# A two-layer hybrid trunk step: x laid out turned and loaded by token groups, squares summed by products with ones, first projections by groups, other ranks of the woven jobs

## The chip, the cores and the metric

The kernel runs on one core of one Trainium2 chip. The metric is device time in microseconds (us) of that core, for one execution of the whole program. Times of a kernel are given as the median of several runs, with the lowest and highest. Traces come from one profiled execution.

## The reference, cut to what matters

One inference step of a trunk of two layers, for a prompt of 1024 tokens and 8 samples of 4 tokens each, so T = 1056 tokens of width D = 1024.

```python
for layer in range(2):
    shift, scale, gate = split(silu(c) @ w_mod[layer] + b_mod[layer])       # c: prompt row, 8 sample rows
    h = rms_norm(x, norm_g[layer]) * (1 + scale) + shift
    if layer == 0:   # sliding-window attention: 16 heads, 4 KV heads of 64, window 128, sinks
        q, k, v, z = split(h @ swa_w_in)
        branch = (attend(q, k, v) * silu(z)) @ swa_w_out
    else:            # gated DeltaNet: 8 q/k heads, 16 v heads of 128, conv of 4 taps, chunks of 64
        xqkv, z, a, b = split(h @ gdn_w_in)
        q, k, v = silu(causal_conv(xqkv))                                    # q, k then l2-normalised
        o = gated_delta(q, k, v, beta(b), decay(a), S0)                      # a state S per head and sample
        branch = (rms_norm(o) * silu(z)) @ gdn_w_out
    x = x + gate * branch
y = rms_norm(x, final_norm_g)
```

Outputs are y, the last keys and values, and the new conv and DeltaNet states.

## The kernel before, in words

**Layout.** Activations lie turned: the width stands on the 128 partitions, in 8 slices (KD = 8, numbered k or e), and the tokens on the columns, in three token groups (`GRP`, L24): columns 0 to 384, 384 to 768, and 768 to 1056, the last 32 of these being the sample tokens. An fp32 product of full precision is made of three products in the faster type fp32r, since each factor is split into a high and a low part: hi·hi, hi·lo and lo·hi (`hhi`, `hlo` of the activations; `wh`, `wl` of the weights).

**Who sets the order.** All instructions go through one helper (`call`, L83), so the profile shows L84 for nearly all of them. The program order on each engine is the order in which the Python code issues them; a planner keeps a model of when each engine comes free (`nc.free`). Loads that must keep an order among themselves go through `queued` (L276) on SyncE's queue (SP). Work that is not on the main line (attention, the chunks of DeltaNet, the splitting of weights, the sample tokens) is written as generators, "jobs". `weave` (L456) puts a job into a list by its rank from the tables `K` and `KR` (lower rank first), and `stages` (L467) tries the list from the front between two matrix products of the main line; a job goes on until its next condition does not hold. So a changed rank changes what stands between which products, not what is computed. `MM` (used at L1243) spaces the steps of the second layer's modulation, `SW` (used at L2378) the products with the sample states S.

**The front** (L282 to L735). `xload` brings x, as it is stored, in nine blocks of up to 128 tokens (512 KB each) into `xt`. `turn_x` (L605) turns a block by eight 128x128 transposes on TensorE, copies the result into `zo` (the turned x) on VectorE and has ScalarE square the block and add up each token's squares (`xss`). The pool of `xt` has `XB` = 14 places, shared with the modulation weights `wm` (eight slices, two loads of 512 KB each, `wmod_load`). `modulation_rows` shapes the conditioning vector `cT`; `modulate(e)` (L638) makes slice e of shift and scale by eight 32-row products with `wm`; `fold(e)` (L649) turns the result to columns, `Sc` and `Sh`. `scale_x` (L618) makes the reciprocal root of all nine blocks at once in small VectorE steps (`sv` to `rsx`); `spread_x(gi)` (L624) spreads it over the partitions by products with the identity and has ScalarE copy it to `rsb`. `hold(n)` (L673) issues n filler products whose result is not used. `shape_h(k)` (L657) makes slice k of the layer's input: `fu` = x · Sc · rsb on VectorE, `hhi` = fu + Sh on ScalarE, `hlo` = the remainder on VectorE, in two spans of prompt columns, and four small steps for the 32 sample columns. `split_w` (L420) makes `wh` on ScalarE, then `wl` on GpSimd. `first_part(k, p_)` (L685) makes slice k's nine products for one of two column blocks, 3 groups by 3 products; 8 slices, 2 column blocks and 9 products are the 144 first projections. The loop over k that issues them computes slice k+1's `shape_h` beside slice k's products and loads weights ahead.

**The middle.** Layer 0's other projections (`project`, L519) with attention woven in; its output product; layer 1's projections with the chunked DeltaNet woven in.

**The last stage** is layer 1's output product, in blocks (`out_block`, L2259) of 48 products of 512 columns, 768 in all, on `h2hi`, `h2lo` (activations) and `ohi`, `olo` (weights). Woven between them is the samples' DeltaNet, a chain: 16 steps with S (`states_times`, L2349: four 32x256 products `S,zq` each, two loads of 512 KB for each step ahead through five places), then `core` (L2403: KQT, U, oH), then `second_half` and `new_states` (L2586, L2601: `U,kb`). The sample rows' own block comes behind the 384th output product.

Of the kernel before, what the change touches and what calls it, by code (L numbers as in the profile page):

```python
# [14 lines left out]
P = 128  # L15
D = 1024
# [198 lines left out]
def body(tc, I, O, cst_ap, dbg=None):  # L215
# [21 lines left out]
    K = {'split': 4, 'add': 3, 'attend': 12, 'turning': 14, 'modulate': 31, 'cached': 9, 'wo': 39, 'turn': 0, 'ahead': 2, 'taps': 2, 'gating': 5, 'decay': 27, 'samples': 9, 'load': 4, 'mod': 9, 'shape': 9, 'decays': 8, 'prepare': 0, 'gather': 30, 'finish': 55, 'states': 21, 'core': 4, 'new': 9}  # L237
    KR = [{'chain': 8, 'output': 3, 'solve': 5, 'invert': 21, 'blocks': 10, 'decayed': 0}, {'chain': 10, 'output': 3, 'solve': 12, 'invert': 10, 'blocks': 35, 'decayed': 40}, {'chain': 33, 'output': 2, 'solve': 22, 'invert': 19, 'blocks': 33, 'decayed': 9}, {'chain': 20, 'output': 21, 'solve': 3, 'invert': 4, 'blocks': 30, 'decayed': 17}, {'chain': 14, 'output': 0, 'solve': 1, 'invert': 17, 'blocks': 31, 'decayed': 11}, {'chain': 3, 'output': 13, 'solve': 6, 'invert': 20, 'blocks': 55, 'decayed': 29}, {'chain': 6, 'output': 1, 'solve': 11, 'invert': 20, 'blocks': 45, 'decayed': 11}, {'chain': 10, 'output': 8, 'solve': 4, 'invert': 28, 'blocks': 40, 'decayed': 44}]
    TB = (3, 6)
    SW = (1, 16)  # L240
# [3 lines left out]
    MM = (0, 20)  # L244
# [4 lines left out]
    XB, FB = 14, 3  # L249
    FH, LATEP = (1, 3), False  # L250
# [11 lines left out]
    gb = cp.tile([P, 64], F32, name="gb")  # L262
# [22 lines left out]
    xts, wms = {}, {}  # L285
# [11 lines left out]
    early = COFF["fold32"][0] + COFF["fold32"][1]  # L297
    cst = cp.tile([P, nkeep], F32, name="cst")
    C = {k: cst[:, o:o + w] for k, (o, w) in COFF.items() if o < nkeep}
    ident = C["ident"]  # L300
    craw = xp.tile([P, KD, 9], F32, name="craw")
    xload(0)
    queued(cst[:, 0:early], cst_ap[:, 0:early])
    xload(1)
    queued(craw.rearrange("p k c -> p (k c)"), I["cgb"][:, 64:136])
    queued(gb, I["cgb"][:, 0:64])
    turns_x = [0, 1, NB, 2, 3, 4, 5, 6, 7]
    for t in turns_x[2:]:
        xload(t)
# [2418 lines left out]
```

## Time and profile before

| | before |
| --- | --- |
| runs, us | 1671.0, 1672.88, 1670.3 (median 1671.0) |
| the profiled execution's own time, us | 1669.87 |
| its span in the trace, us | 1668.1 |
| mean granted TensorE clock | 0.988 |
| instructions in the trace | 30471 |
| HBM read, written | 147.54 MB, 49.84 MB: 118 GB/s over the span |

How to read the lines that follow. In the page, an engine's row gives busy us, the share of the span, and the number of instructions; PEld is the weight load of TensorE, which overlaps its products. In the busy times by stretches, a row has the stretch, its length, then the busy us (and the instructions) of PE, PEld, DVE, ACT and POOL, the granted TensorE clock, the mean busy share of the 16 DMA engines, and the GB/s that they moved. In the rows in order of time stand the start, the duration in us, the engine, the line, the operation with what it writes and reads, the shape, the number of trace records, and in square brackets the idle time of the engine just ahead of the row and what ended it. Where one row stands for several products, its start is that of the first, and a fp32 product that isn't split counts two records.

### The profile page before, as it was taken

The page shows a single profiled execution, that of the slowest core. Times are in us where ns is not written, and L with a number is a line of the kernel's source. Part 1 is how long each engine was busy: PE and PEld are TensorE (multiplying, and loading weights), DVE is VectorE, ACT ScalarE, POOL GpSimd, SP SyncE. Part 2 cuts the span into 40 slices and gives each one's busy share as a digit, 9 for nine tenths or more (in the row PEclk, how much of TensorE's full clock was granted, in tenths as well). Part 3 has the DMA queues.
Part 4 walks back from the last instruction along what each step waited for, and adds up shares of the span by engine and source line. Part 5 has one row for each costly group of instructions (what it writes and reads, how often), then busy time and mean ns, then how long its engine had stood idle before and what let it go on. Part 6 is the DMA issues. An engine that isn't in the chain of part 4 may idle for free.

```text
span 1668.1 us, 30471 instructions
## 1 busy us (share of the span) xinstructions
PE 1594.5 (96%) x10552; PEld 1411.4 (85%) x10552; DVE 1224.1 (73%) x3809; ACT 844.8 (51%) x2422; POOL 221.8 (13%) x289
## 2 busy tenths in 40 slices
PE   8999999999999999989999999999999999888896
PEld 6888888978678999979999889999999987466775
DVE  6726776665666687887988878787898967277777
ACT  4635565444344664546653754656655745133332
POOL 1300000003222001020010102001010033132231
PEclk9999999999999999999999999999999999998998
DMA  9442111124332423133313224232242157853784
GB/s 353 142 142 77 56 49 51 64 72 141 108 128 96 125 61 97 48 104 93 110 51 101 82 74 118 65 113 71 68 132 55 62 167 200 262 192 121 243 271 154
DMA packets 190891, 196.80 MB, mean 118 GB/s; under 512 B 86432, under 2 KB 137472, under 8 KB 190688
## 3 DMA queue, kind: packets, MB, share of 16 engines
q1 hardware_dynamic: 190736, 194.84, 38.0%
q8 instruction: 84, 1.38, 0.3%
q14 instruction: 71, 0.58, 0.1%
HBM read 147.54 MB, written 49.84 MB: 118 GB/s over the span
## 4 chain that ended last, share of the span: by engine, by line
PE 49%; DVE 8%; DMA 4%; ACT 3%; issue 1%; POOL 0%; SPq 0%; POOLq 0%; ACTq 0%; DVEq 0%
PE ps_pj L84 31%; PE ps_lg L84 7%; PE ps_mi L84 6%; PE ps_ob L84 3%; PE ps_tr L84 3%; DMA S<-in_states 1%; DMA of<-gTd 1%; DVE rst L84 1%; DVE y L84 1%; DVE S L84 1%; DVE rsw L84 0%; ACT L84 0%; DVE oH L84 0%; ACT jc L84 0%; DMA xt<-x2d 0%
## 5 line engine op out<-in xcount | busy, mean ns | idle before, releaser
L84 PE MATMUL ps_pj<-h2lo,wh 128*128 128x384 f32 (+1 forms) x1128 | 379.8, 337 | 0.0
L84 PE MATMUL ps_pj<-h2hi,wl 128*128 128x384 f32 (+1 forms) x1128 | 378.4, 335 | 0.9 <-DVE wl L84 0.9
L84 PE MATMUL ps_pj<-h2hi,wh 128*128 128x384 f32 (+1 forms) x1128 | 378.4, 335 | 0.0
L84 PEld LDWEIGHTS ps_pj<-h2hi,wl 128*128 128x128 f32 x1128 | 212.5, 188 | 4.1 <-DVE wl L84 1.2
L84 PEld LDWEIGHTS ps_pj<-h2hi,wh 128*128 128x128 f32 x1128 | 212.5, 188 | 2.9
L84 PEld LDWEIGHTS ps_pj<-h2lo,wh 128*128 128x128 f32 x1128 | 212.4, 188 | 2.8
L84 POOL TENSOR_TENSOR Xd<-Xc,cst 32x128 f32<-32x128 f32 x128 | 68.0, 531 | 425.3 <-DMA Xc<-Xdd 195.7
L84 PE MATMUL ps_pj<-hlo,wh 128*128 128x384 f32 (+1 forms) x376 | 124.3, 331 | 0.1
L84 PE MATMUL ps_pj<-hhi,wh 128*128 128x384 f32 (+1 forms) x376 | 124.4, 331 | 0.0
L84 PE MATMUL ps_pj<-hhi,wl 128*128 128x384 f32 (+1 forms) x376 | 123.4, 328 | 0.0
L84 DVE TENSOR_TENSOR wl<-wr,wh 128x512 fp32r<-128x512 f32 x120 | 83.2, 693 | 16.1 <-ACT wh L84 15.5
L84 POOL TENSOR_TENSOR xt<-xt,y 128x512 f32<-128x512 f32 (+1 forms) x48 | 65.4, 1364 | 219.6 <-DVE y L84 199.5
L84 DVE SCALAR_TENSOR_TENSOR vT<-XR,cT,vT 128x384 f32<-128x384 f32 (+1 forms) x144 | 80.8, 572 | 10.4 <-ACT vT L84 9.6
L84 ACT CAST wh<-wr 128x512 fp32r<-128x512 f32 x128 | 78.6, 616 | 16.4 <-PE ps_pj L84 14.8
L84 PEld LDWEIGHTS ps_pj<-hlo,wh 128*128 128x128 f32 x376 | 70.7, 188 | 11.2 <-issue 10.2
L84 PEld LDWEIGHTS ps_pj<-hhi,wh 128*128 128x128 f32 x376 | 70.7, 188 | 4.1 <-issue 3.8
L84 PEld LDWEIGHTS ps_pj<-hhi,wl 128*128 128x128 f32 x376 | 70.7, 188 | 2.8 <-issue 2.7
L84 DVE TENSOR_TENSOR X<-X,tmp 128x126 f32<-128x126 f32 (+22 forms) x248 | 63.8, 257 | 8.5
L84 ACT ACTIVATE qe<-ps_mi,Eg 128x128 f32<-128x128 f32 x112 | 35.0, 363 | 68.8 <-PE ps_mi L84 68.8
L84 ACT COPY XR<-ps_pj 128x384 f32<-128x384 f32 (+1 forms) x96 | 43.3, 451 | 52.1 <-PE ps_pj L84 51.8
L84 DVE TENSOR_TENSOR tmp<-X 128x126 f32<-128x126 f32 (+22 forms) x248 | 62.3, 251 | 7.7 <-POOL X L84 3.9
L84 ACT ACTIVATE prob<-prob,nm 128x256 f32<-128x256 f32 (+1 forms) x128 | 62.2, 488 | 9.6 <-DVE nm L84 9.4
(542 smaller groups left out, 3910.9 us busy)
## 6 DMA issues: line engine op xcount, KB each, us to landing
wr<-in_gwb SPq DMA_DIRECT2D x96, 256.0 KB
S<-in_states SPq DMA_DIRECT2D x40, 256.0 KB
xt<-in_x_prompt SPq DMA_DIRECT2D x16, 512.0 KB
wm<-in_wm SPq DMA_DIRECT2D x16, 512.0 KB
wr<-in_winb SPq DMA_DIRECT2D x32, 256.0 KB
wmod<-in_w_mod SPq DMA_DIRECT2D x32, 256.0 KB
wm<-in_w_mod SPq DMA_DIRECT2D x32, 256.0 KB
DP<-gcr SPq DMA_DIRECT2D x64, 128.0 KB
```

The lines of the kernel that those rows point to most:

```text
L84: inst = fn(*args, **kwargs)
```

## The change

It has three parts, and nothing else differs.

**The front's data.** The host lays x out turned, in two arrays: `xT0` (the first two token groups, four loads of two slices each, 786 KB) and `xT1` (the third group, two loads of four slices). They are loaded straight into `zo`; the transposes, their copies and `xt` as a place of x are gone. The early constants, the norm and bias rows and the conditioning vector come as one load, `erl`. The pool that is now of `wm` alone has 12 places.

**The front's work.** `square_x` squares slices of the turned x, odd ones on VectorE and even ones on ScalarE; `total` sums them over the partitions by products with a column block of ones (`w32`), each into one of four 32-row strips; `scale_tot` copies the sums, and `scale_x` makes 1/32 of the strips' sum by products of one column, six blocks of tokens at first and three later, and then the reciprocal root as before. `shape_h` takes a range of columns, and its `hlo` half is issued separately (`rest`); the sample columns have `shape_s`. `first_part` takes the groups it is to do, and its order is hi·hi, lo·hi, hi·lo. The loop over k gives way to a list written out by hand: groups 0 and 1 of the first slices ahead of group 2. Of the two calls of `hold`, with one and three products, the first stays.

**The ranks.** Six entries of `K`, six of `KR`, `SW` and `MM` have other values.

```diff
-    K = {'split': 4, ... 'cached': 9, ... 'load': 4, ... 'shape': 9, ... 'states': 21, ... 'new': 9}
+    K = {'split': 25, ... 'cached': 29, ... 'load': 6, ... 'shape': 5, ... 'states': 14, ... 'new': 4}
...
-    SW = (1, 16)
+    SW = (4, 19)
-    MM = (0, 20)
+    MM = (1, 17)
-    XB, FB = 14, 3
-    FH, LATEP = (1, 3), False
+    XB, FB = 12, 4
...
-    def xload(t):
-        xts[t] = xp.tile([P, D], F32, tag="xt", name="xt", bufs=XB)[0:P if t < NB else TS]
-        queued(xts[t], xp_rows[t * P:(t + 1) * P] if t < NB else xs_rows)
+    def xload(gi, i):
+        w = zo[0].shape[1] // (2 - gi)
+        queued(zo[i * w // 4][:, i * w % 4:i * w % 4 + w, (0, 2 * GW)[gi]:(2 * GW, T)[gi]], I[f"xT{gi}"][i])
...
-    def turn_x(n, t):
...
-                nc.tensor.transpose(pt[:, j * parts:(j + 1) * parts], xts[t][:, k * P:(k + 1) * P],
-                                    ident[0:parts, 0:parts])
-            nc.vector.tensor_copy(zo[kk][:, :, t * P:t * P + parts],
-                                  pt[:, 0:4 * parts].rearrange("p (q t) -> p q t", q=4))
-        nc.scalar.activation(sq[0:parts], xts[t], AF.Square, accum_out=xss[0:parts, n:n + 1])
+    def square_x(q, gis):
+        a, b = GRP[gis[0]][0], GRP[gis[-1]][1]
+        sqs = {}
+        for e in (2 * q, 2 * q + 1):
+            x = zo[e // 4][:, e % 4, a:b]
+            sqs[e] = xp.tile([P, 2 * GW], F32, tag="sq", name="sq", bufs=4)[:, 0:b - a]
+            if e % 2:
+                nc.vector.tensor_tensor(sqs[e], x, x, ALU.mult)
+            else:
+                nc.scalar.activation(sqs[e], x, AF.Square)
+        def total():
+            for gi in gis:
...
+                for e, sq in sqs.items():
+                    j = (e + 2 * gi) % 4
+                    nc.tensor.matmul(sums[gi][32 * j:32 * j + 32, 0:b1 - a1], w32[:, 0:32], sq[:, a1 - a:b1 - a],
+                                     start=(e < 4), stop=(e >= 4), skip_group_check=True)
...
+    def scale_x(gis):
...
+            nc.tensor.matmul(pss[0:n, j:j + 1], tot[:, t * P:t * P + n], w32[:, 32:33], start=True, stop=True)
...
-            for n, (x, y) in enumerate(((hi, hhi), (hi, hlo), (lo, hhi))):
+        for n, (x, y) in enumerate(((hi, hhi), (lo, hhi), (hi, hlo))):
+            for gi in gis:
...
+    scale_tot((0, 1))
+    scale_x((0, 1))
+    hold(1)
+    modulate(0)
+    fws[0] = split_w(fraws.pop(0))
+    fold(0)
+    spread_x(0)
+    spread_x(1)
+    shape_h(0, 0, 768)
+    us.pop((0, 0))()
+    modulate(1)
+    wmod_load(6)
+    square_x(0, (2,))
+    first_part(0, 0, (0, 1))
+    square_x(1, (2,))
+    fold(1)
+    shape_h(1, 0, 768)
+    fws[1] = split_w(fraws.pop(1))
+    totals[0, 2]()
+    modulate(2)
...
```

What stands on the engines now. First TensorE at its start. In before, this is what follows sixteen groups of transposes of x like the first two rows (`cst` holds the identity):

```order
L84 MATMUL ps_tr<-cst,xt 128x128 x4
L84 MATMUL ps_ob<-cst,xt 128x128 x4
L84 MATMUL ps_mi<-wm_122,cT 32x256 x4
L84 MATMUL ps_mi<-wm_124,cT 32x256 x4
L84 MATMUL ps_mi<-wm_128,cT 32x256 x4
L84 MATMUL ps_mi<-wm_130,cT 32x256 x4
L84 MATMUL ps_mi<-cst,ma 128x32 x2
L84 MATMUL ps_mi<-zo,cst 128x384
L84 MATMUL ps_lg<-cst,rsx 128x128 x3
L84 MATMUL ps_ob<-cst,rsx 128x128 x3
L84 MATMUL ps_lg<-cst,rsx 128x128 x2
L84 MATMUL ps_lg<-cst,rsx 128x32
```

In after, the same engine's first instructions are these (`sq` are the squares, `w_98` the ones, `erl` holds the identity):

```order
L84 MATMUL ps_lg<-sq,w_98 32x384 x16
L84 MATMUL ps_tr<-w_98,tot 128x1 x6
L84 MATMUL ps_mi<-zo,erl 128x384
L84 MATMUL ps_mi<-wm_107,cT 32x256 x4
L84 MATMUL ps_mi<-wm_109,cT 32x256 x4
L84 MATMUL ps_mi<-erl,ma 128x32 x2
L84 MATMUL ps_ob<-erl,rsx 128x128 x3
L84 MATMUL ps_tr<-erl,rsx 128x128 x3
L84 MATMUL ps_mi<-wm_113,cT 32x256 x4
L84 MATMUL ps_mi<-wm_115,cT 32x256 x4
L84 MATMUL ps_pj<-hhi,wh 128x384 x2
L84 MATMUL ps_pj<-hhi,wl 128x384 x2
```

The 72 transposes are replaced by sixteen sums and six one-column products; only one modulation stands ahead of the spread, which covers two token groups, and a projection of two groups follows the second modulation.

Second, SyncE's queue at the start, in before (`craw` and `gb` are the conditioning vector and the norm and bias rows):

```order
L84 DMA xt<-in_x_prompt 128x1024
L84 DMA cst<-in_cst 128x160
L84 DMA xt<-in_x_prompt 128x1024
L84 DMA craw<-in_cgb 128x72
L84 DMA gb<-in_cgb 128x64
L84 DMA xt<-in_x_sample 32x1024
L84 DMA xt<-in_x_prompt 128x1024 x6
L84 DMA wm_122<-in_wm 128x1024
L84 DMA wm_124<-in_wm 128x1024
L84 DMA wr<-in_win 128x512
L84 DMA wm_128<-in_wm 128x1024
L84 DMA wm_130<-in_wm 128x1024
```

And the same queue in after:

```order
L84 DMA zo<-in_xT 128x2x768
L84 DMA erl<-in_erl 128x296
L84 DMA zo<-in_xT 128x2x768 x3
L84 DMA wm_107<-in_wm 128x1024
L84 DMA wm_109<-in_wm 128x1024
L84 DMA wr<-in_win 128x512
L84 DMA wm_113<-in_wm 128x1024
L84 DMA wm_115<-in_wm 128x1024
L84 DMA wm_117<-in_wm 128x1024
L84 DMA wm_119<-in_wm 128x1024
L84 DMA zo<-in_xT 128x4x288 x2
L84 DMA cst<-in_cst 128x488
```

The weights of the first two modulations now stand behind two token groups of x instead of three, and the third group behind the weights of slice 2.

Third, TensorE in the last stage, where the products with S begin. In before (`h2hi`, `h2lo`, `ohi`, `olo`: output products; a row of `S,zq` is half a step):

```order
L84 MATMUL ps_pj<-h2hi,ohi 128x512
L84 MATMUL ps_lg<-S_17060,zq 32x256 x2
L84 MATMUL ps_lg<-S_17062,zq 32x256 x2
L84 MATMUL ps_pj<-h2hi,olo 128x512
L84 MATMUL ps_lg<-S_17064,zq 32x256 x2
L84 MATMUL ps_lg<-S_17066,zq 32x256 x2
L84 MATMUL ps_pj<-h2lo,ohi 128x512
L84 MATMUL ps_pj<-h2hi,ohi 128x512
L84 MATMUL ps_pj<-h2hi,olo 128x512
L84 MATMUL ps_pj<-h2lo,ohi 128x512
```

In after:

```order
L84 MATMUL ps_pj<-h2hi,olo 128x512
L84 MATMUL ps_lg<-S_17051,zq 32x256 x2
L84 MATMUL ps_lg<-S_17053,zq 32x256 x2
L84 MATMUL ps_lg<-S_17055,zq 32x256 x2
L84 MATMUL ps_lg<-S_17057,zq 32x256 x2
L84 MATMUL ps_pj<-h2lo,ohi 128x512
L84 MATMUL ps_tr<-erl,vo 128x128 x4
L84 MATMUL ps_pj<-h2hi,ohi 128x512
L84 MATMUL ps_pj<-h2hi,olo 128x512
L84 MATMUL ps_pj<-h2lo,ohi 128x512
```

Two steps with S stand back to back in after. Counted in output products ahead of each of the 16 steps, before has 97, 98, 106, 107, 116, 121, 125, 160, 163, 167, 172, 176, 181, 185, 190, 194, and after 98, 98, 104, 105, 116, 116, 149, 149, 157, 158, 166, 167, 175, 176, 184, 190. The transposes of KQT stand behind 283 output products in before and 277 in after, the first product of U with `kb` behind 358 and 352, the product of `oH` behind 384 in both; from the 482nd on the rows are the same.

On GpSimd two memsets of the attention's cached values stand behind the front in after and not at the start, since the memory that they write is the front's until then. From about 600 to 1350 us TensorE's rows are nearly the same in both kernels, and the number of instructions is close everywhere: TensorE's queue has 8977 in before and 8935 in after, VectorE's 3811 and 3822, ScalarE's 1991 and 1997, GpSimd's 294 and 297, SyncE's 973 and 968.

More of the change, by code (lines that the diff above doesn't have):

```diff
@@ L695, in body @@
     wmod_load(1)
-    for n, t in enumerate(turns_x):
-        turn_x(n, t)
-        if n == 1:
-            modulation_rows()
-    queued(cst[:, early:], cst_ap[:, early:nkeep])
     wmod_load(2)
+    xload(1, 0)
+    xload(1, 1)
+    queued(cst, cst_ap[:, early:nkeep])
     first_load(1)
-    ma = modulate(0)
-    scale_x(0, 9)
-    ma1 = modulate(1)
-    fold(0, ma)
-    fws[0] = split_w(fraws.pop(0))
-    hold(FH[0])
-    for gi in range(3):
-        spread_x(gi)
-    shape_h(0)
-    fold(1, ma1)
```

255 lines of the change are left out of this document (182 added, 73 removed).

## The prediction

> **What bounds the kernel now.** I read the share of busy time first, then the busy time by stretches, then TensorE's rows in order of time, and last the rows of the engines it waits for.
>
> ```profile
> PE 1594.5 (96%) x10552; PEld 1411.4 (85%) x10552; DVE 1224.1 (73%) x3809; ACT 844.8 (51%) x2422; POOL 221.8 (13%) x289
> ...
> 0.00:10.00 10.00, 4.21 (x20) 3.51 (x20) 2.33 (x4) 4.66 (x8) 2.44 (x11) 1.00 0.84 273
> 10.00:20.00 10.00, 9.77 (x71) 8.88 (x70) 8.34 (x15) 7.19 (x15) 0.04 (x1) 1.00 1.03 407
> 20.00:30.00 10.00, 8.79 (x51) 6.37 (x51) 5.17 (x20) 3.62 (x8) 2.72 (x3) 0.83 1.03 406
> 30.00:40.00 10.00, 9.92 (x78) 7.62 (x77) 9.35 (x21) 4.44 (x11) 1.38 (x1) 1.00 0.98 383
> 40.00:50.00 10.00, 10.00 (x83) 8.51 (x83) 9.07 (x22) 4.27 (x9) 1.38 (x1) 1.00 0.14 44
> ...
> 100.00:150.00 50.00, 50.00 (x359) 44.12 (x358) 30.55 (x120) 24.14 (x80) 0.00 (x0) 1.00 0.31 108
> ```
>
> TensorE (PE) is busy for 1594.5 of 1668.1 us, and from 100 us on a stretch is 50.00 of 50.00: whatever the front saves is kept behind it, since the work there is limited by TensorE and merely starts earlier. In the front the last two columns matter: for 40 us the DMA engines are full at about 0.407 MB/us (2.73 MB in the first 10 us), and TensorE's busy time there is partly filler and transposes. So the price of the change is read from one question: when do the real projections start, and how long do they then take?
>
> ```profile
> 20.57 0.64 PE L84 MATMUL ps_mi<-wm,cT 128*32 128x256 f32 x8 [0.80 <-DMA wm<-in_wm]
> 21.85 0.64 PE L84 MATMUL ps_mi<-wm,cT 128*32 128x256 f32 x8 [0.64 <-DMA wm<-in_wm]
> ...
> 22.98 1.65 PE L84 MATMUL ps_mi<-zo,cst 128*128 128x384 f32 x2
> 24.42 1.49 PE L84 MATMUL ps_lg<-cst,rsx 128*128 128x128 f32 x6
> 26.71 0.94 PE L84 MATMUL ps_lg<-cst,rsx 128*128 128x128 f32 x6
> 28.05 2.18 PE L84 MATMUL ps_mi<-zo,cst 128*128 128x384 f32 x6
> 29.78 0.63 PE L84 MATMUL ps_pj<-hhi,wh 128*128 128x384 f32 x1
> 30.48 0.44 PE L84 MATMUL ps_pj<-hlo,wh 128*128 128x384 f32 x1
> ...
> 45.94 1.07 PE L84 MATMUL ps_mi<-wm,cT 128*32 128x256 f32 x16
> 50.47 1.07 PE L84 MATMUL ps_mi<-wm,cT 128*32 128x256 f32 x16
> ...
> 62.91 0.40 PE L84 MATMUL ps_tr<-hlo,wh 128*128 128x288 f32 x1 [0.45 <-DVE hlo L84]
> 64.61 0.30 PE L84 MATMUL ps_ob<-hhi,wl 128*128 128x288 f32 x1
> ```
>
> The first projection stands at 29.78 and the last of the sixteen (eight slices of the model width, two column blocks) ends at 64.91, so 35.1 us. Inside, one slice takes 4.53 us (45.94 to 50.47) with almost no wait named. Two of the rows ahead of it, 22.98 and 28.05 (the products of zo with the identity), are filler from `hold`.
>
> **The change part by part: when the first projection starts.** The loads first. In before, the second half of the modulation weights of slice 1 stands behind 6.83 MB in the queue; at 0.407 MB/us these have moved by 10 + (6.83 - 2.73) / 0.407 = 20.1 us, and the row at 21.85 starts when it lands: 1.8 us behind the count. In after, the first two token groups of x (four loads of 128x2x768) and the early constants are 3.30 MB, so they land at 11.4 + 1.8 = **13.2 us**; the weights of slice 1 (5.66 MB) at 19.0, the third group (7.89 MB) at 24.5, the last modulation weights (14.15 MB) at 39.9. All but the first lie ahead of their use below, so the DMA sets only the start.
>
> From 13.2 us a chain follows, priced by the nearest rows:
>
> ```profile
> 4.73 1.09 PE L84 MATMUL ps_pj<-cst,xt 128*128 128x128 f32 x4 [4.73 <-DMA cst<-in_cst]
> 17.73 0.60 PE L84 MATMUL ps_tr<-cst,xt 128*128 128x128 f32 x4
> ...
> L84 DVE TENSOR_TENSOR wl<-wr,wh 128x512 fp32r<-128x512 f32 x120 | 83.2, 693 | 16.1 <-ACT wh L84 15.5
> ...
> 20.24 0.16 DVE L84 TENSOR_SCALAR sv<-xss 128x9 f32<-128x9 f32 x1
> 22.49 0.17 DVE L84 SCALAR_TENSOR_TENSOR rsx<-rst,rsw 128x9 f32<-128x9 f32 x1
> 26.46 0.62 DVE L84 SCALAR_TENSOR_TENSOR fu<-zo,Sc,rsb 128x384 f32<-128x384 f32 x1 [2.89 <-ACT rsb L84]
> ...
> 22.55 0.37 ACT L84 COPY ma<-ps_mi 128x256 f32<-128x256 f32 x1 [2.35 <-PE ps_mi L84]
> 25.95 0.48 ACT L84 COPY rsb<-ps_lg 128x384 f32<-128x384 f32 x1 [2.50 <-PE ps_lg L84]
> ```
>
> The last square on 768 columns of VectorE (DVE) is 1.5 times the 693 ns row, 1.0 us. The products with ones were not in before. Four of them work on separate 32-row strips, as the modulation's do (the 20.57 row: 0.64 us for four of 256 columns), so 0.96 us for 384 columns, 1.9 at the half clock. Copy of the sums 0.48. Six products with one column are bounded by the transposes, which load the same 128x128 operand: 0.9 (17.73 row) to 1.6 (4.73 row). Then the branches: on VectorE the reciprocal root, 20.24 to 22.66, 2.4 us; on TensorE one filler product (0.7 to 1.65), modulation 0 (1.07 to 2.1), ScalarE's copy 0.37, the fold (0.6 to 1.0). TensorE's branch is the longer one. After it the spread (0.94 to 1.49), its copy 0.48, the scaling 0.62 and the bias on ScalarE, about 0.62 more. At the full clock the sum is 13.2 + 1.0 + 0.96 + 0.48 + 0.9 + (0.73 + 1.07 + 0.37 + 0.63) + 0.94 + 0.48 + 0.62 + 0.62 = **22.0**; at half the clock **26.6**. The 72 transposes, which cost TensorE from 4.73 to 18.8 us, are gone, but they lay beside the loads, so they count only through this chain. I take 24.0: cold for the sums, warm for about half of the rest. That is 5.8 us ahead of 29.78.
>
> **How long the projections then take.** The same 144 projection products, six modulations and the folds take 35.1 us in before. Added between them: one fold (0.4), eight sums over 288 columns, two side by side (four times 0.72, of which two pairs stand together: 2.2), three one-column products (0.4) and the spread of the third group (0.5), 3.5 us. Lost are the two stalls seen above, 30.48 - 29.78 instead of 0.18 and 0.45: 1.0 us. Sum 37.6 us, so the front ends at 24.0 + 37.6 = **61.6**.
>
> VectorE is the second bound, and here it is as near:
>
> ```profile
> 31.24 0.28 DVE L84 TENSOR_SCALAR Sc<-ps_mi,bS,gb 128x9 f32<-128x9 f32 x1
> 34.68 1.29 DVE L84 TENSOR_TENSOR hlo<-fs,hhi 128x32 fp32r<-128x32 f32 x1
> 35.89 0.28 DVE L84 TENSOR_SCALAR Sc<-ps_mi,bS,gb 128x9 f32<-128x9 f32 x1
> 39.33 0.18 DVE L84 TENSOR_TENSOR hlo<-fs,hhi 128x32 fp32r<-128x32 f32 x1
> 40.00 0.28 DVE L84 TENSOR_SCALAR Sc<-ps_mi,bS,gb 128x9 f32<-128x9 f32 x1 [0.49 <-PE ps_mi L84]
> ...
> 34.54 1.38 POOL L84 TENSOR_TENSOR wl<-wr,wh 128x512 fp32r<-128x512 f32 x1 [4.92 <-ACT wh L84]
> ```
>
> A slice is 4.65 us (31.24 to 35.89) where GpSimd (POOL) splits a weight meanwhile, and 4.11 - 0.49 = 3.62 where it doesn't: four of each, 33.1 us. Added are four squares of 288 columns (0.39 each, 1.6), a second reciprocal root (2.4) and 16 more instructions, since the columns come in three pieces and not in two (an estimate of 1.0); taken away are three of the four small sample steps of slices 0 to 3 (1.4). From the first scaling at about 22.8 that is 36.7 us, so 59.5, and 2.1 us of projections follow the last slice: 61.6 again. Two engines with the same sum mean that a stall on either is no longer covered, so no more than this is taken: **-3.3 us** against 64.91, with ends at -5.3 (first product at 22.0, end 59.6) and -0.5 (every GpSimd product blocks VectorE, below).
>
> The rows at 34.54 and 34.68 show VectorE's small difference (0.18 us at 39.33) held up until GpSimd's product ends. The Trainium skill's page "SBUF — State Buffer" says of the shared port pair that a VectorE operation with two SBUF inputs and a GpSimd operation that reads SBUF exclude each other, and the second fully blocks; this row agrees. By that rule the squares and the root's steps, which have two such inputs, would be held up as well. With it the sum is the first rival's, 1669.1; without it, 1666.3.
>
> **The rest.** The multiset of the other instructions is unchanged; from about 600 to 1350 us TensorE's order is nearly word for word the same, so nothing is booked there. The ranks move work in the attention part (both signs open, booked at 0 with 2 either way) and in the last stage:
>
> ```profile
> 1414.83 0.39 PE L84 MATMUL ps_pj<-h2hi,olo 128*128 128x512 f32 x1
> 1415.06 0.39 PE L84 MATMUL ps_pj<-h2lo,ohi 128*128 128x512 f32 x1
> ...
> 1424.47 1.30 PE L84 MATMUL ps_lg<-S,zq 128*32 128x256 f32 x8 [2.48 <-DMA S<-in_states]
> 1435.43 0.63 PE L84 MATMUL ps_lg<-S,zq 128*32 128x256 f32 x4 [1.16 <-DMA S<-in_states]
> 1527.75 0.63 PE L84 MATMUL ps_lg<-cst,oH 128*128 128x128 f32 x4 [2.60 <-DVE oH L84]
> ...
> 1420.00:1440.00 20.00, 16.31 (x85) 9.19 (x86) 4.68 (x14) 3.06 (x9) 1.48 (x2) 0.91 0.90 281
> ```
>
> Of the 768 output products, 384 stand ahead of the product of oH in both kernels, and TensorE waits there 2.60 us for the sample chain. In after the chain's earlier members stand six output products sooner (the KQT transposes behind 277 of them, not 283; the first product of U behind 352, not 358). One is 0.23 us (1414.83 to 1415.06), so the wait shrinks by 6 x 0.23 = **1.4 us**. It is nothing if the loads of S set the chain's pace, and I keep 0 as the other end.
>
> Sum: the profiled execution took 1669.87 us (span 1668.1); 1669.87 - 3.3 - 1.4 = 1665.2. The median of the runs is 1671.0, 1.1 above that execution, so **1666.3**.
>
> **The rivals.** *VectorE is the bound and blocked.* For: its sum equals TensorE's. If the two sample products and one more split on GpSimd (2.8 us) block as the 34.68 row was, the front ends at 64.4, gain 0.5: 1669.1. Against: GpSimd is idle for most of the stretch.
>
> *TensorE stays at half clock.* The row of one microsecond in before shows it:
>
> ```profile
> 24.00:25.00 1.00, 1.00 (x4) 0.70 (x4) 0.00 (x0) 0.00 (x0) 0.80 (x1) 0.50 0.99 393
> ```
>
> The granted clock is 0.50 there, after the gaps at 20.57 and 21.85. In after TensorE has less to do before the first projection, so the chain may run at its cold price, 26.6; the front ends at 64.2, and the time is 1668.9. The Trainium skill's page "TensorE: Matmul & The Clock Gate", in the part on the HAM clock gate, says that the clock is halved by default and released only after a window of sustained work of some 3.4 us; it speaks against dropping the transposes, and the row agrees that gaps are followed by the half clock. By that rule the time is 1668.9, without it 1666.3.
>
> *Slower: the loads of S.* In after the products with S stand in pairs of steps, eight in a row, every nine output products. A pair needs 1.05 MB; at 0.281 MB/us (the 1420 row) that is 3.7 us, while nine products are 2.1 us. Four such places short by 1.6 us are 6.5 us, and the 1.4 us are lost: 1669.87 - 3.3 + 6.5 + 1.1 = 1674.2. It decides against the change from 3.3 us of added waiting. Against it: before waits for S in the same stretch already, and its single steps ask for the same bytes.
>
> *More than forecast.* The chain is warm (-5.3), the wider spacing of the S steps ends the two waits for S quoted (3.6), and the 1.4 hold: 1669.87 - 10.3 + 1.1 = 1660.7.
>
> **How the numbers follow.** Forecast 0.42 (its own range 1663.5 to 1668.5), blocked VectorE 0.15, cold clock 0.12, slow S loads 0.15, more than forecast 0.16. The measurement tells about 0.2% (3.3 us) from no change, so faster means below 1667.7. Nearly all of the forecast, the last case and a fifth of the two weak ones are faster, 0.58; the rest of these is within, 0.26; slower 0.16. The range takes in the five cases with 2 us for the attention part beyond the outer ones on the fast side: 1657 to 1675.
>
> **What would show it.** Right: the first projection near 24 us, the last near 61.6, the granted clock at 1.00 from the first on, the wait for oH about 1.2 us. Wrong: VectorE busy above 9.5 of 10 us between 30 and 60 with TensorE waiting for hlo or hhi; a half clock past 24 us; waits for S that add up to much more than 5 us behind 1400; or a new wait in the attention part, which this sum books at nothing.

## The result, and the profile after

| | before | after |
| --- | --- | --- |
| runs, us (7 each, on one chip) | median 1671.0 (1665.71 to 1679.87) | median 1660.59 (1658.88 to 1666.54) |
| profiled execution, us | 1669.87 | 1658.88 |
| its span, us | 1668.1 | 1657.1 |

The ratio is 0.9941, with an interval of 0.9916 to 0.9965: 9.9 us faster (6 to 14). A second set of runs of the same kernel on another chip gave 0.992 (0.990 to 0.994). The time lies within the predicted range and 5.7 us under the forecast of 1666.3. Where the time went is not where the prediction had put it, so the stages come first. The table gives the start of the first product of its kind in each profile: `wvh` is the first product of v's weights, a little behind the first projections, `kw0` the first of layer 1, "projections end" the end of layer 1's last one.

| stretch | before, us | after, us | difference | predicted |
| --- | --- | --- | --- | --- |
| start to first projection | 29.78 | 27.61 | -2.2 | -5.8 |
| first projection to `wvh` | 49.66 | 52.48 | +2.8 | +2.5 |
| `wvh` to `kw0` (attention, output of layer 0) | 438.69 | 436.65 | -2.0 | 0 |
| `kw0` to projections end | 852.89 | 853.49 | +0.6 | 0 |
| projections end to first output product | 14.52 | 7.97 | -6.6 | 0 |
| first output product to the product of oH | 142.21 | 141.00 | -1.2 | -1.4 |
| from there to the end of the span | 140.35 | 137.90 | -2.5 | 0 |
| sum | 1668.1 | 1657.1 | -11.0 | -4.7 |

The front gave nothing in this pair of profiles (+0.6 by `wvh`); all the gain lies behind it, where only the ranks differ. The stretches of single profiles scatter by some us (below), so the column of differences is a first reading. First the page and the busy times by stretches of after, with the columns of before (PE, PEld, DVE, ACT, POOL, granted clock, DMA share, GB/s):

```profile
PE 1592.9 (96%) x10540; PEld 1406.3 (85%) x10540; DVE 1216.1 (73%) x3820; ACT 842.5 (51%) x2419; POOL 221.7 (13%) x292
```

```profile
10.00:20.00 10.00, 8.60 (x42) 3.90 (x38) 3.79 (x11) 2.17 (x3) 0.48 (x2) 1.00 1.03 408
...
30.00:40.00 10.00, 9.62 (x87) 7.75 (x80) 8.49 (x29) 4.48 (x11) 1.73 (x2) 1.00 1.03 403
40.00:50.00 10.00, 9.65 (x90) 7.49 (x91) 9.09 (x22) 6.19 (x14) 1.81 (x3) 1.00 0.03 10
```

TensorE's busy time is the same to 1.6 us (1594.5 before), so 9.4 of the 11.0 us are time in which it waited. Between 10 and 20 us TensorE looks busy (8.60 of 10), as it did with the transposes (9.77); what it is busy with shows in its rows in order of time, up to the last of the first projections:

```profile
13.43 1.64 PE L84 MATMUL ps_lg<-sq,w 128*32 128x384 f32 x8 [0.32 <-ACT sq L84]
15.71 2.69 PE L84 MATMUL ps_tr<-w,tot 128*128 128x1 f32 x12 [0.65 <-ACT tot L84]
18.27 1.63 PE L84 MATMUL ps_mi<-zo,erl 128*128 128x384 f32 x2
19.83 1.94 PE L84 MATMUL ps_mi<-wm,cT 128*32 128x256 f32 x16
23.13 1.63 PE L84 MATMUL ps_ob<-erl,rsx 128*128 128x128 f32 x6
27.61 0.74 PE L84 MATMUL ps_pj<-hhi,wh 128*128 128x384 f32 x2
...
65.81 0.29 PE L84 MATMUL ps_tr<-hlo,wh 128*128 128x288 f32 x1
```

The modulation takes 1.94 us here and 1.07 in before's front at 45.94: the chain runs at about half speed from the first sum to shortly before the first projection, and the first projections end at 66.1, not at 61.6.

Second, the place where most of the time was won in this pair of profiles: behind layer 1's last projection. Here a chain of states goes from chunk to chunk (S with kT on TensorE, `vo` on VectorE, `vo` with UZ on TensorE, `us` on VectorE, `us` with ktok on TensorE, and S again), and VectorE and ScalarE also split the output weights `wr` into `h2hi` and `h2lo` for the next stage. The rows of before, in order of time:

```profile
1373.76 0.62 ACT L84 CAST h2hi<-wr 128x512 fp32r<-128x512 f32 x1 [2.49 <-DMA wr<-in_gdn_w_out]
1374.41 0.69 DVE L84 TENSOR_TENSOR h2lo<-wr,h2hi 128x512 fp32r<-128x512 f32 x1 [2.32 <-ACT h2hi L84]
1375.03 0.60 DVE L84 SCALAR_TENSOR_TENSOR vo<-ps_mi,nEg,vo 128x128 f32<-128x128 f32 x2
1375.42 0.75 PE L84 MATMUL ps_ob<-vo,UZ 128*128 128x128 f32 x4 [2.51 <-DVE vo L84]
...
1377.65 1.32 DVE L84 TENSOR_TENSOR h2lo<-wr,h2hi 128x512 fp32r<-128x512 f32 x1 [1.69 <-ACT h2hi L84]
1378.89 0.60 DVE L84 TENSOR_SCALAR us<-ps_ob,sd 128x128 f32<-128x128 f32 x2
1379.54 1.22 PE L84 MATMUL ps_mi<-us,ktok 128*128 128x256 f32 x2 [3.37 <-DVE us L84]
...
1385.54 0.58 PE L84 MATMUL ps_pj<-h2hi,ohi 128*128 128x512 f32 x1
```

Read from the bottom: the first output product stands at 1385.54, behind a product of `us` that waited 3.37 us; `us` stood on VectorE behind a split `h2lo` that waited for ScalarE's cast, and the cast waited for the load of `wr`. The same chain of waits stands ahead of `vo` (2.51, 2.32, 2.49). Then the busy times of before in the same place:

```profile
1374.00:1378.00 4.00, 0.75 (x4) 0.56 (x4) 1.90 (x5) 2.38 (x6) 0.87 (x1) 1.00 0.74 249
1378.00:1382.00 4.00, 2.46 (x7) 2.10 (x8) 2.68 (x6) 0.89 (x2) 0.42 (x1) 0.51 1.02 249
1382.00:1386.00 4.00, 4.00 (x11) 2.12 (x10) 0.50 (x3) 1.71 (x5) 0.00 (x0) 0.64 0.91 258
```

After the waits the granted clock is 0.51 and 0.64 for 8 us. In after, one such wait is left, and the granted clock behind it stays at 1.00:

```profile
1371.96 0.91 DVE L84 TENSOR_TENSOR h2lo<-wr,h2hi 128x512 fp32r<-128x512 f32 x1 [1.55 <-ACT h2hi L84]
1372.80 0.60 DVE L84 TENSOR_SCALAR us<-ps_ob,sd 128x128 f32<-128x128 f32 x2
1373.45 0.70 PE L84 MATMUL ps_mi<-us,ktok 128*128 128x256 f32 x2 [2.77 <-DVE us L84]
...
1378.20 0.48 PE L84 MATMUL ps_pj<-h2hi,ohi 128*128 128x512 f32 x1
```

```profile
1374.00:1378.00 4.00, 3.59 (x15) 2.10 (x14) 2.75 (x7) 3.22 (x13) 0.09 (x1) 1.00 0.93 240
```

In TensorE's program two products of `us` with ktok stand between the last projection and the first output product in before, one in after: the chain is one step ahead when the projections end. Third, the last stage in after: the waits for S, for KQT and for oH (before had 3.81 at KQT, and 2.60 at oH).

```profile
1418.19 1.33 PE L84 MATMUL ps_lg<-S,zq 128*32 128x256 f32 x8 [1.72 <-DMA S<-in_states]
1441.95 0.63 PE L84 MATMUL ps_lg<-S,zq 128*32 128x256 f32 x4 [2.85 <-DMA S<-in_states]
1452.98 0.63 PE L84 MATMUL ps_lg<-S,zq 128*32 128x256 f32 x4 [0.94 <-DMA S<-in_states]
...
1487.78 1.68 PE L84 MATMUL ps_lg<-erl,KQT 128*128 128x128 f32 x8 [3.26 <-DVE KQT L84]
...
1519.20 0.63 PE L84 MATMUL ps_lg<-erl,oH 128*128 128x128 f32 x4 [1.45 <-DVE oH L84]
```

The waits for S sum to 5.5 us, and to 5.2 in before (2.48, 1.16 and three under 0.75).

### The profile page after: what moved, and what is told of

It reads as the page before. It is cut to its first block, busy times and chain, and to the rows that moved or that the text cites. A ratio compares the mean times of both kernels' runs of the same rounds, so it can differ in the third digit from the quotient of the medians.

```text
span 1657.1 us, 30435 instructions
## 1 busy us (share of the span) xinstructions
PE 1592.9 (96%) x10540; PEld 1406.3 (85%) x10540; DVE 1216.1 (73%) x3820; ACT 842.5 (51%) x2419; POOL 221.7 (13%) x292
## 4 chain that ended last, share of the span: by engine, by line
PE 50%; DVE 7%; DMA 4%; ACT 3%; issue 1%; POOL 0%; SPq 0%; POOLq 0%; ACTq 0%; DVEq 0%
PE ps_pj L84 32%; PE ps_lg L84 6%; PE ps_mi L84 6%; PE ps_ob L84 3%; PE ps_tr L84 2%; DMA S<-in_states 1%; DMA xt<-x2d 1%; DVE S L84 1%; DMA out_y_p<-xt 1%; ACT jc L84 1%; DVE rst L84 1%; DVE y L84 0%; ACT L84 0%; DMA x2d<-xt 0%; DVE oH L84 0%
## 5 line engine op out<-in xcount | busy, mean ns | idle before, releaser
L84 ACT CAST wh<-wr 128x512 fp32r<-128x512 f32 x128 | 78.7, 616 | 16.3 <-PE ps_pj L84 15.6
L84 ACT COPY XR<-ps_pj 128x384 f32<-128x384 f32 (+1 forms) x96 | 43.5, 453 | 53.3 <-PE ps_pj L84 52.9
```

Of the source, the lines that this page charges most:

```text
L84: inst = fn(*args, **kwargs)
```

## Experiments

All ratios are to the kernel before, from runs on the same chip, five rounds each. The chip was one for `front_only`, `ranks_only`, `chunk_ranks_back` and `warm_start` (median of before 1673.8 us), a second for `chunk_only`, `splits_pool`, `samples_back` and `attention_back` (1674.31), and a third for `after_again`, `warm_no_hold`, `mm_back` and `split_cached_back` (1672.49). Times of single profiles scatter by some us, so stretches are compared over all profiles that share an order. A half-clock window below is a stretch of about 3.4 us in which the granted clock is 0.50, so that 1.7 us of clock are lost.

### The front alone and the ranks alone

TensorE's rows behind the front are before's in the first kernel and after's in the second, so the two halves of the change are separate. `front_only` is after with (the tables in short)

```diff
-    K, KR, SW, MM = (those of after)
+    K, KR, SW, MM = (those of before)
```

and `ranks_only` is before with the opposite edit.

> The new front with the ranks of before (K, KR, SW, MM), so that from the front's end on the instructions stand in the order of before. Theory 1, the gain is all the ranks' and the front is worth nothing: the front ends at 66.0 us as in the profile after (64.9 before), the gap of 5.9 us on TensorE at 1372 to 1380 is back, and the time is 1671 to 1673 us. Theory 2, the front is worth some us that the later stages show: 1666 to 1668 us.

> The front of before with the new ranks; behind the front TensorE's rows are those of after. Theory 1 (the ranks carry all, the front ends 1.1 us later than before's): the time is that of after less about 1, 1659 to 1660.5 us. Theory 2 (both halves carry): 1664 to 1667 us.

`front_only`: 1673.74 us, ratio 0.9995 (0.9979 to 1.001). `ranks_only`: 1662.08 us, ratio 0.9926 (0.9906 to 0.9947). The expectations were written for a chip on which before takes 1671.0 us; by the ratios the times there would be 1670.2 and 1658.6. The ranks carry the gain, and the front none that can be measured: theory 1, within 1 us of its figures, and theory 2 falls.

What of the front? Twelve profiles besides the two with warmed products (below) answer that: eight with the new front, four with the old.

| | first projection, us | first projection to `wvh`, us | `wvh`, mean, us |
| --- | --- | --- | --- |
| old front (before, chunk_only, splits_pool, ranks_only) | 27.88 to 30.67, mean 29.2 | 49.66 to 49.71 | 78.9 |
| new front (eight profiles) | 23.05 to 27.83, mean 25.9 | 52.5 to 52.9 | 78.6 |

The new front starts 3.3 us sooner and takes 3.1 us longer from there: 0.2 us, nothing.

### The ranks of the chunk jobs

`chunk_ranks_back` is after with KR of before; `chunk_only` is before with KR of after. The edit of `chunk_only`, with two of its six entries shown, is this; that of `chunk_ranks_back` is the opposite one:

```diff
-    KR = [{'chain': 8, ... {'chain': 10, ... 'blocks': 40, 'decayed': 44}]
+    KR = [{'chain': 1, ... {'chain': 10, ... 'blocks': 2, 'decayed': 44}]
```

> The changed kernel with KR alone (the ranks of the chunk jobs of layer 1) as in before. If KR closes the gap of 5.9 us at 1372 to 1380 us and the half clock behind it: the gap returns and the time is 1665.5 to 1668 us. If the gain is that of K and SW (the samples' jobs in the last stage): no gap, 1660 to 1662 us.

> The kernel before with KR alone (the ranks of the chunk jobs) as in after. At the end of layer 1's projections TensorE's rows are then after's: one product of us with ktok behind the last projection and ahead of the output products, where before has two. If these ranks carry the larger part of the gain: of the two waits there (2.51 and 3.37 us in before) one is left, of 2 to 3.3 us, the half clock behind them is shorter, and the ratio to before is 0.996 to 0.997 (5 to 7 us). If the gain needs K and SW as well: 0.998 to 1.000.

`chunk_ranks_back`: ratio 0.997 (0.9954 to 0.9987). The two waits are back (2.04 and 3.33 us), with the half clock behind them; by the ratio the time is 1666.0 us where before takes 1671.0, as expected. `chunk_only`: 0.9979 (0.9965 to 0.9992), 3.5 us: less than the 5 to 7 expected, more than nothing. In its profile one wait is left at that place:

```profile
1377.67 0.70 PE L84 MATMUL ps_mi<-us,ktok 128*128 128x256 f32 x2 [2.73 <-DVE us L84]
1380.44 1.98 PE L84 MATMUL ps_lg<-modG,selt 128*128 128x512 f32 x4 [0.61 <-DMA selt<-in_cst]
```

From the projections' end to the first output product the ten profiles with the new KR have 7.8 to 10.3 us, mean 8.8; the three with the old one and no other edit there 12.6 to 14.5, mean 13.5. Of these 4.7 us some is given back: up to the first product with S it is 43.3 and 47.0 us, 3.7. So the stretches agree with the 3.5 us of `chunk_only`.

### The blocked VectorE taken away by itself

`splits_pool` is before with the splits of the first eight output weights on GpSimd alone.

```diff
-                eng = "gpsimd" if k % 2 else "vector"
+                eng = "gpsimd" if k % 2 or k < HK else "vector"
```

> The kernel before with all its ranks; only the splits h2lo of the first eight output weights all go to GpSimd (half of them stood on VectorE). Theory: the waits of 2.51 and 3.37 us behind the last projection are the chain of states held up on VectorE behind such a split, which waits for the cast and so for the load of wr. Then they shrink to under 2.5 us in all, the half clock behind them goes, and the ratio is 0.996 to 0.998 (3.5 to 6 us). Rival: the chain's own steps, or the loads, take that long anyway, or the output products now wait for GpSimd's splits: the first output product stands as far behind the last projection as before (14.5 us), 0.999 to 1.002.

1680.8 us, ratio 1.0033 (1.0018 to 1.0049): slower. The rows behind the last projection:

```profile
1379.39 0.70 PE L84 MATMUL ps_mi<-us,ktok 128*128 128x256 f32 x2 [1.42 <-DVE us L84]
1382.04 0.81 PE L84 MATMUL ps_mi<-uo,DP 128*128 128x128 f32 x4 [1.51 <-ACT uo L84]
1384.15 1.22 PE L84 MATMUL ps_ob<-vo,UZ 128*128 128x128 f32 x4 [0.45 <-DVE vo L84]
...
1390.62 0.47 PE L84 MATMUL ps_pj<-h2hi,ohi 128*128 128x512 f32 x1
```

The two waits of 5.9 us became these three of 3.4 and one of 1.08 (for S on VectorE, at 1390.17), 4.5 us in all, where less than 2.5 was expected. Two products of `us` with ktok still stand there, and the first output product comes 13.1 us behind the projections' end (14.5 in before, 8.0 in after), as the rival said. New waits of 3.2 us (for `vo` on ScalarE) and 3.0 (for `y` on VectorE) follow 37 and 42 us behind that end. Taking the split off VectorE alone mostly moves the waits. That the number of chain steps left over is what counts fits these rows and those of `chunk_only`, but no run changes that number alone.

### The ranks of the attention part

`attention_back` is after with MM and three ranks of before, `mm_back` with MM alone, `split_cached_back` with the three ranks alone.

```diff
-    MM = (1, 17)
+    MM = (0, 20)
-    K = {'split': 25, ... 'cached': 29, ... 'shape': 5, ...}
+    K = {'split': 4, ... 'cached': 9, ... 'shape': 9, ...}
```

> The changed kernel with MM and the ranks 'split', 'cached' and 'shape' as in before; TensorE's rows differ from after's in the attention part and not behind 500 us. If these ranks give what the profiles show (wvh to kw0 438.7 us in before, 436.7 in after): that stretch is 2 us longer again, TensorE's waits in it are 6 to 8 us where after has 3.3, and the ratio is 0.995. If they do nothing: 436 to 437 us and 0.994.

> The changed kernel with MM alone (the spacing of the second layer's modulation among the attention's products) as in before; TensorE's rows differ in the first two thirds of the attention part. The nine profiles have the stretch from wvh to the first product of layer 1 (kw0) at 438.7 to 443.5 us with the old attention ranks and 436.3 to 439.3 with the new. If MM is what counts, this profile has 439 to 443 us and the ratio is 0.995 to 0.998; if not, 436 to 439 us and that of after_again.

> The changed kernel with the ranks 'split', 'cached' and 'shape' as in before; TensorE's rows differ in the last third of the attention part and in the output product of layer 0. If these ranks are what counts in the attention part: wvh to kw0 in 439 to 443 us and a ratio of 0.995 to 0.998; if not, 436 to 439 us and that of after_again.

`attention_back`: 0.996 (0.9941 to 0.998). `split_cached_back`: 0.9932 (0.9916 to 0.9948), not told apart from after's 0.992 on the same chip. `mm_back`: 0.9999 (0.9978 to 1.0019): with MM alone taken back no gain can be measured any more, which is more than was expected. In its profile TensorE waits three times in the attention part:

```profile
155.08 1.09 PE L84 MATMUL ps_mi<-erl,prob 128*128 128x128 f32 x6 [1.26 <-DVE prob L84]
227.70 0.96 PE L84 MATMUL ps_mi<-erl,prob 128*128 128x128 f32 x4 [0.36 <-DVE prob L84]
233.53 0.44 PE L84 MATMUL ps_mi<-erl,kx 128*128 128x128 f32 x2 [1.83 <-ACT pT L84]
```

The three waits, 3.4 us, stand in all six profiles with the old MM, to within 0.1 us, and in none of the eight with the new one. And in three of the six a half-clock window follows the third wait, as here:

```profile
234.00:235.00 1.00, 1.00 (x9) 0.49 (x8) 1.00 (x6) 0.41 (x2) 0.00 (x0) 0.86 0.52 188
235.00:236.00 1.00, 1.00 (x7) 0.61 (x4) 0.39 (x4) 0.37 (x1) 0.00 (x0) 0.50 0.45 144
236.00:237.00 1.00, 1.00 (x7) 1.00 (x6) 0.00 (x0) 0.40 (x1) 0.00 (x0) 0.50 0.03 6
237.00:238.00 1.00, 1.00 (x6) 1.00 (x5) 0.60 (x1) 0.18 (x1) 0.00 (x0) 0.50 0.03 6
238.00:239.00 1.00, 1.00 (x7) 0.75 (x8) 0.96 (x8) 0.21 (x1) 0.00 (x0) 0.94 0.00 0
```

The columns sum to 1.7 us lost. Waits and one such window are 5.1 us, and the stretch from `wvh` to `kw0` has 438.7 to 446.1 us with the old MM, mean 441.5, and 436.3 to 439.3 with the new, mean 437.2: 4.2 us. (`attention_back` has 443.5 there, `mm_back` 446.1 and `split_cached_back` 437.4.) The 13 us of `mm_back` against after are not all explained by this. Its mean granted clock over 12 runs is 0.9846, that of after over 6 runs beside it 0.9902: one less the clock, times the mean time, is 25.8 and 16.3 us, so the clock would be 9.5 of the 12.1 us between the means. In `mm_back`'s profile further half-clock windows stand at 371, 391, 722, 979 and 1385 us; the profile after has some too, near 365 and 715. At 371 and 391 TensorE's order is not that of after: the products with the cached keys `KT` stand elsewhere among the projections, and the last of them waits for its load, with a window behind it:

```profile
390.93 0.64 PE L84 MATMUL ps_lg<-KT,qz 64*32 64x128 f32 x16 [1.83 <-DMA KT<-in_keysT]
```

In after, and in `attention_back`, which has the old MM too, the last of these products waits for nothing. So old MM with the new other ranks gives an order of its own there, with a cost that before doesn't have; this is one reason why `mm_back` can lose more than `attention_back`. At 722, 979 and 1385 the order is after's as far as the rows show, and whether the old MM brings those windows, or these runs fell so, is open. The new MM alone on the ranks of before was not run.

### The ranks of the samples' jobs

`samples_back` is after with

```diff
-    SW = (4, 19)
+    SW = (1, 16)
-    K = {... 'load': 6, ... 'states': 14, ... 'new': 4}
+    K = {... 'load': 4, ... 'states': 21, ... 'new': 9}
```

> The changed kernel with SW and the ranks 'states', 'new' and 'load' as in before; TensorE's rows differ from after's only in the last stage. By the prediction's term the wait for oH grows from 1.45 to about 2.6 us, and the time is 1.4 us above after's, so a ratio to before of 0.995 where after has 0.994; by the profile after, where the last stage (first product with S to the last output product) is 2.6 us shorter than in before, up to 2.6 us, 0.996. If these ranks do nothing: 0.994, and the wait for oH stays under 1.6 us.

0.9933 (0.9907 to 0.9958), no difference from after that can be told.

```profile
1492.64 1.97 PE L84 MATMUL ps_lg<-erl,KQT 128*128 128x128 f32 x8 [4.80 <-DVE KQT L84]
1525.48 0.63 PE L84 MATMUL ps_lg<-erl,oH 128*128 128x128 f32 x4 [1.41 <-DVE oH L84]
```

The wait for oH stays at 1.41; the one for KQT grows from 3.26 to 4.80. `chunk_only`, which has SW of before, also waits 1.38 us for oH, and `chunk_ranks_back`, with SW of after, 1.79. So either set of ranks shrinks the wait for oH from 2.60, but not by the same order. With the old KR and the new SW TensorE's rows have KQT, U and oH behind 277, 352 and 384 output products, as in after; with the new KR and the old SW (`samples_back`, `chunk_only`) behind 271, 336 and 371. So `samples_back` doesn't bring back the order of before, and the growth of the wait that was expected of it could not show.

### TensorE kept busy from the start

`warm_start` is after with products of a zeroed tile; `warm_no_hold` is the same without `hold(1)`.

```diff
+    warm = xp.tile([P, 384], F32, name="warm")
+    nc.vector.memset(warm, 0.0)
+    wps = psb("mi")
...
+            nc.tensor.matmul(wps[:, 0:384], warm[:, 0:P], warm, start=True, stop=True)
+    warmer(6)
     square_x(0, (0, 1))
     totals[0, 1]()
+    warmer(2)
     square_x(1, (0, 1))
     totals[1, 1]()
+    warmer(1)
     modulation_rows()
     square_x(2, (0, 1))
     totals[2, 1]()
+    warmer(1)
```

> The changed kernel with ten products of a zeroed tile added (128x384, result unused): six ahead of the first sums of squares, four between them, so that TensorE works from about 1 us on. If the half clock sets the chain to the first projection: the pair of hold takes 0.7 to 0.8 us where it took 1.63, the first projection stands at 22.5 to 23.5 us (27.61), the front ends at 61.5 to 63 us (65.9) and the time is 1656.5 to 1658 us. If VectorE bounds the front: the first projection comes forward, the end does not (above 64.5 us), 1659.5 to 1661 us.

> The changed kernel itself, beside the next three on the same chip. The six profiles with the new front have the first projection at 23.1 to 27.8 us, by how soon TensorE's products take their full-clock time, and the stretch from there to the first product of v's weights (wvh) at 52.5 to 52.9 us. If the half clock of the front is a matter of each execution, this profile lies anywhere in that range; ratio 0.992 to 0.995.

> warm_start (ten products of a zeroed tile ahead of and between the first sums) without the one filler product of hold. Clock theory: first projection at 22.2 us or a little sooner, wvh at 75 us, and 2 to 5 us faster than after_again (ratio 0.988 to 0.992). If VectorE or the loads bound the front: wvh at 77 us or later, and no faster than after_again.

`warm_start`: 1661.17 us, ratio 0.9903 (0.9877 to 0.9929); `after_again`: 1658.97 us, 0.992 (0.990 to 0.994); `warm_no_hold`: 1660.26 us, 0.9916 (0.9896 to 0.9937). Beside `after_again` the last is neither faster nor slower. In the profile of `warm_start` the whole chain is at full speed:

```profile
15.38 1.47 PE L84 MATMUL ps_tr<-w,tot 128*128 128x1 f32 x12 [0.65 <-ACT tot L84]
16.72 0.89 PE L84 MATMUL ps_mi<-zo,erl 128*128 128x384 f32 x2
...
22.36 0.44 PE L84 MATMUL ps_pj<-hhi,wh 128*128 128x384 f32 x1 [0.20 <-ACT hhi L84]
```

The filler takes 0.89 us where after has 1.63, the first projection stands at 22.36, the front's end at 61.2, and `wvh` at 75.17 where the eight profiles have 78.6 on average: the clock theory holds, and VectorE does not bound the front. (By the ratio the time is 1654.8 where before takes 1671.0, below the 1656.5 to 1658 expected.) `after_again` has its first projection at 25.96, within the range. In `warm_no_hold` the products are slow again from 18.63 on, and a step of the reciprocal root on VectorE is held up:

```profile
18.63 1.06 PE L84 MATMUL ps_mi<-erl,ma 128*128 128x32 f32 x4 [0.49 <-ACT ma L84]
19.17 1.26 POOL L84 TENSOR_TENSOR wl<-wr,wh 128x512 fp32r<-128x512 f32 x1 [8.09 <-ACT wh L84]
19.18 1.27 DVE L84 SCALAR_TENSOR_TENSOR rst<-rst,sv 128x6 f32<-128x6 f32 x1
20.71 1.65 PE L84 MATMUL ps_ob<-erl,rsx 128*128 128x128 f32 x6 [1.02 <-DVE rsx L84]
...
25.41 0.62 PE L84 MATMUL ps_pj<-hhi,wh 128*128 128x384 f32 x2
```

The spread of 1.65 us is 0.91 at full speed in `warm_start`. The root's step takes 1.27 us beside GpSimd's split of a weight; the same step takes 0.17 in `warm_start`, where the split starts at 19.65, behind the root. Without the filler the modulation, and so ScalarE's copy and cast ahead of the split, come sooner and the split meets the root: the spread waits 1.02 us for it. So the expectation, 22.2 us, had taken the filler for lost time, and `wvh` at 77.75 falls under its second case. What set off the half clock ahead of the step is not shown; the waits there are 0.65 and 0.49 us. The 3.5 us that `warm_start` gains in the front are not resolved in the times: its interval overlaps that of `ranks_only` on the same chip, and no version here is shown to be faster than after.

## Why the prediction was right and wrong

**What held, and what was luck.** The direction and the range held, but the sum behind them did not. The front's term of -3.3 came out at about 0, the ranks' term of -1.4 at about -12, and the two errors have opposite signs: that the total is only 5.7 us from the forecast is luck. The loads set only the start, as said: in the profile after no wait of TensorE between the first sum and `wvh` is for a load. With TensorE at full speed the sum of the chain holds too: 22.36 us in `warm_start`, where 22.0 was summed. The first projections take 52.5 to 52.9 us to `wvh` where the old front takes 49.7, 3.1 longer; the prediction summed 2.5. The rival of slow loads of S fell: the waits for S sum to 5.5 us, with steps in pairs, where before has 5.2. The rival of a blocked VectorE did not decide the time of after: VectorE is busy for 8.49 and 9.09 of 10 us between 30 and 50, under the 9.5 named as a sign, and `warm_start` moved `wvh` by 4.9 us against after. But the blocking itself is real, and `warm_no_hold` met it in the reciprocal root.

**The step on the front's start.** "I take 24.0: cold for the sums, warm for about half of the rest." The profile after has 27.61, above the cold end of the range (26.6); eight profiles give 23.05 to 27.83, mean 25.9. The mechanism (half the clock) was named, as a rival of 0.12, and it is what after's profile shows; over the eight profiles the first projection lies between the full-clock price and a little over the cold one. The term for the six products with one column was too small at either speed: 2.69 us measured in after and 1.47 in `warm_start`, where 1.6 and 0.9 were booked from the transposes. One reading was off, at no cost to the sum: the 0.7 us from 29.78 to 30.48 in before, booked as a stall, hold the last filler product of `hold` (29.75, 0.49 us), which the change drops. With the start 3.3 us sooner and the length 3.1 longer, the term of -3.3 is about 0.

```profile
18.00:20.00 2.00, 2.00 (x8) 0.92 (x12) 1.32 (x8) 0.00 (x0) 0.00 (x0) 1.00 0.99 391
```

That is the profile after in the middle of the slow chain: the column of the granted clock says 1.00 while the filler at 18.27 takes 1.63 us. The prediction's test "the granted clock at 1.00 from the first on" could not have shown the fault; durations of one known product do.

**The step on the ranks.** "The ranks move work in the attention part (both signs open, booked at 0 with 2 either way) and in the last stage", and between projections and output nothing was booked at all. The ranks gave 0.9926, 12.4 us of 1673.8: the term that was mis-sized is this one, booked at -1.4. The rows were there to see: the profile before has waits of 1.26, 0.35 and 1.81 us in the attention part, the last of them here, and of 2.51 and 3.37 behind the projections, and the order of the changed kernel shows one chain step fewer between the last projection and the first output product.

```profile
232.65 0.44 PE L84 MATMUL ps_mi<-cst,kx 128*128 128x128 f32 x2 [1.81 <-ACT pT L84]
```

Such a wait costs its length and, in some executions, a half-clock window behind it; neither was in the sum.

**The last stage.** The wait for oH is 1.45 us, predicted 1.2. The -1.4 came out as -1.2 between the first output product and oH, but this is one pair of profiles: over all fourteen that stretch has 139.1 to 147.8 us, so the agreement says little. The six output products themselves are borne out: with the old KR, SW and its ranks move KQT and U by six (`chunk_ranks_back`). In the nine profiles of that order the wait is 1.26 to 1.84 us, and 2.60 in before and 2.61 in `front_only`, so it shrinks by 0.8 to 1.3. But KR shrinks the same wait without them, by another order, and the times of `samples_back` show no gain of SW and its ranks.

**The figure of the case "more than forecast"**, 1660.7, is close to the result, but its reasons (a warm chain, fewer waits for S) are not what happened.

**What stays open** is the size of MM's part: 4.2 us by stretches of the profiles, and 3 to 13 by the times (`attention_back`'s 0.996 and `mm_back`'s 0.9999, against 0.9941 and 0.992 of after).

## What to carry to other kernels

Price a wait on the busiest engine as its length plus the half-clock window that may follow it (here 1.7 us, in some executions), and look for both in the order where a stage ends: count the steps of a serial chain that are left over when the work that covers it runs out. Filler products that look like waste may hold the clock, or keep other engines' work apart; before a stage of TensorE's is dropped or shortened, ask what keeps it busy until the next real product, and what will start sooner. Where a change has two halves, make each alone first: here one half was worth nothing and the other all of it, and the profile pair alone could not tell, since the same order scatters by several us.

## What the runs showed of the hardware

A wait shorter than its consequence: behind a single wait of 1.83 us at 232 us the granted clock is 0.50 for 3.4 us (the five rows of `mm_back` sum to 1.7 us lost, at half the clock), and that in three of the six profiles that have this wait. Near 715 us, behind waits of 0.8 to 2.2 us, such a window comes in ten of the fourteen profiles. Near 970, behind one wait for S of 0.9 to 2.9 us, it comes in the four where that wait is longest (2.39 to 2.91). The Trainium skill's page "TensorE: Matmul & The Clock Gate", in the part on the HAM clock gate, gives a free-running window of some 3.4 us and says that the number of slow products at a kernel's start varies from run to run; the length agrees, and the scatter is of the same kind. It names an idle window of about 3.4 us as what halves the clock; here waits of half that length were enough in some executions, and the measurement decides.

Over the 66 runs of before that stood beside these experiments the mean granted clock is 0.9853 and the mean time 1673.9 us, so by the same product 24.6 us of clock are missing in each. Not all of that is lost time: in the profile before the clock is 0.50 from 1660 to 1668 us too, where TensorE has no work left (0.00 us busy). Nor is all of it counted, since the column shows 1.00 in the slow start. Between those runs time and clock have a correlation of -0.77, so much of the scatter of this kernel goes with how many of these windows an execution meets; which brings the other is not shown.
